# Layer 0's group norm: the root of 512 sums taken as 128 rows of 4, moved by transfers through DRAM

## The chip, the cores and the metric

The kernel runs on one core of a Trainium2 chip. The metric is device time in microseconds for one execution; the times are medians of several runs. The core has five engines with instruction queues of their own, each worked off in order: TensorE (PE in the profile, with its weight loads as PEld), VectorE (DVE), ScalarE (ACT), GpSimd (POOL) and SyncE (SP), which here only issues transfers.

## What is computed

A trunk of two layers over 1024 tokens of width 1024. Layer 0 mixes tokens by differential attention, layer 1 by latent attention; each is followed by a gated MLP with a causal convolution. The change lies in layer 0's attention, whose core is:

```python
def block(args):
    qb, blk = args
    sc = jnp.einsum('bqhcd,bkhcd->bhcqk', qb, k).astype(jnp.float32) * scale
    p = masked_softmax(sc, chunk_mask(blk, s)[None, None, None])
    a = p[:, :, 0] - lam * p[:, :, 1]
    return jnp.einsum('bhqk,bkhe->bqhe', a.astype(v.dtype), v)

o = from_blocks(lax.map(block, (to_blocks(q), jnp.arange(nb))))
o = rms_norm(o, subln_g) * (1.0 - lambda_init)
return o.reshape(b, s, D_MODEL) @ w_o
```

There are 8 heads; each has two softmaxes over the keys ("components"), subtracted with the weight lam. The group norm is the `rms_norm` over the 128 values of one head and one token: each value is divided by the root of the mean of the head's 128 squares plus 1e-6, then multiplied by a gain.

## The kernel before

The kernel is written with a tile framework: the program gives instructions in an order of priority, and a planner, which simulates the engines with costs of its own, sets the order on each engine and places all waits. Some regions are kept in the written order (`manual_schedule`), among them the part of the output projection in which PE and DVE run `project_rest`.

Values are 32-bit floats; to keep precision a matmul operand is split into a high part (`hi`, a rounded copy on ACT, L127) and a residue (`lo`, a subtraction on DVE or POOL, L130), and a product is three matmuls (`mm3`, L119 to L121).

Layer 0's attention goes through 32 steps: 8 heads with 4 pairs of query blocks each (p = 0 to 3, 256 queries in a step). `steps` interleaves them: in turn t it makes the scores and softmaxes of step t, turns and multiplies those of step t-1 by the values (`product`), and runs `finish` of step t-2. In between go the units that project the next queries, keys and values: they accumulate in the one PSUM bank "u" (L119 to L121 with `u<-s,s`), and are taken out by `rope` (shuffle L237, products L238 to L240) or, for values, by an ACT copy (L560). `weigh` divides the softmaxes by their sums: the reciprocal (L1578) on DVE, the second component's scale times -lam on ACT (L1579), the first component's rows on POOL or ACT (L147, L149), and their sum on DVE (L1581).

A half of a head's output, 128 values by 512 tokens, is complete after the steps p = 1 and p = 3; so there are 16 norms. `product` of such a step squares the output twice on ACT (L1599, L1600) and takes the residue on POOL (L130, `h<-h,h`). `finish`, a turn later, sums over the 128 rows by two matmuls with a matrix of ones (L1609, L1610), after which each of the 128 rows of the PSUM bank holds the same 512 sums; `rsqrt` (L170) takes 1 over the root of the whole 128x512 tile by Identity, Ln, Exp and Square on ACT (L174 to L177) and a correcting step on DVE (L178, L179); DVE multiplies with output and gain (L1613), and SP stores the tile to DRAM (L1614).

The tiles live in named places. The outputs `o` rotate over the places h2 and h3, and the tiles of the norm (squares, high part, residue, result, two temporaries) over the ring `fin` of h4 to h7. A tile that takes a place waits until all users of the tile before are done.

Elsewhere in the kernel the root of a norm is taken by POOL with a power of -0.5 (`root`, L167).

The output projection reads the stored halves back in blocks of 128 tokens (`project`, load L593, high part L127, residue L130): `project_first` with heads 0 to 3, which the planner may mix into the last attention steps, then `project_rest` with heads 4 to 7, in the order of blocks 0, 4, 1, 5, 2, 6, 3, 7. Block 4 is the first one that needs the second half of head 7. Weights are fetched by SP ahead of use (L135).

Of the kernel before, what the change touches and what calls it, by code (L numbers as in the profile page):

```python
# [10 lines left out]
F32 = mybir.dt.float32  # L11
F32R = mybir.dt.float32r
AF = mybir.ActivationFunctionType
ALU = mybir.AluOpType
# [4 lines left out]
P = 128  # L19
# [37 lines left out]
class Trunk:  # L57
# [40 lines left out]
    def ring(self, *places):  # L98
        return Ring(self, *places)
# [67 lines left out]
        nc.gpsimd.tensor_tensor(r, s, self.mhalf, ALU.pow)  # L167
        return r

    def rsqrt(self, ring, r, x, scale):  # L170

        nc = self.nc
        v, t = ring([P, 512]), ring([P, 512])
        nc.scalar.activation(v, x, AF.Identity, bias=self.eps, scale=scale)  # L174
        nc.scalar.activation(t, v, AF.Ln)
        nc.scalar.activation(r, t, AF.Exp, scale=-0.5)
        nc.scalar.activation(t, r, AF.Square)  # L177
        nc.vector.scalar_tensor_tensor(t, t, -0.5, v, ALU.mult, ALU.mult)  # L178
        nc.vector.scalar_tensor_tensor(r, t, 1.5, r, ALU.add, ALU.mult)  # L179

    def turn_blocks(self, src, dst):

        n = src.shape[-1] // P
        ps = self.bank()
        for k in range(n):
            self.nc.tensor.transpose(ps[:, k * P : (k + 1) * P], src[:, k * P : (k + 1) * P], self.ident)
        v = ps[:, : n * P].rearrange("p (k s) -> p k s", s=P)
        self.hi(dst(0), v)
        self.lo(dst(1), v, dst(0))
# [91 lines left out]
    def steps(self, attend, units, prepare, n, apart=False):  # L281


        steps = []
        for t in range(n + 2):
            now = before = None
            u = []
            if t < n:
                now = attend(t)
                steps.append(now)  # L290
                prepare(t)
                u = units(t)
                now.scores(0)
            if 0 < t <= n:
                before = steps[t - 1]
            alone = u[:-1] if apart else []
            if alone:
                u = u[-1:]
            self.run(alone or u, 2 if alone else 1)
            if before:  # L300
                before.turn()
            self.run(alone)
            if now:
                now.weigh(0)
                now.scores(1)
            self.run(u)
            if before:
                before.product()
            if now:
                now.weigh(1)  # L310
            if t >= 2:
                steps[t - 2].finish()


    def diff_attention(self, o_d, prefetch):
        nc, a = self.nc, self.a
# [5 lines left out]
        R = SimpleNamespace(  # L322
            k=self.ring("u0", "u1", "u2"), qh=self.ring("u3", "u4"), v=self.ring("u5", "u6", "u7"),
            P=self.ring("u8", "u9", "u10", "u11", "u12"), pT=self.ring("u13", "u14", "u15"),
            o=self.ring("h2", "h3"), fin=self.ring("h4", "h5", "h6", "h7"),
            rope=self.ring("h8", "h9", "h10", "h11"),
        )

# [25 lines left out]
        x, r = [], {}  # L354
# [1177 lines left out]
class DaStep(Step):  # L1532
# [40 lines left out]
    def weigh(self, j):  # L1573

        k, nc, l = self.k, self.k.nc, self.l[j]
        p0, p1 = self.probs[j]
        w = k.stat()
        nc.vector.reciprocal(l, l)  # L1578
        nc.scalar.mul(w, l[:, 1:2], k.neglam)  # L1579
        k.scale(p0, l[:, 0:1], "P" if self.p < 2 else "A")  # L1580
        nc.vector.scalar_tensor_tensor(p0, p1, w, p0, ALU.mult, ALU.add)  # L1581
        self.probs[j] = p0
# [20 lines left out]
    def finish(self):  # L1603

        k, nc = self.k, self.k.nc
        if not self.last:
            return
        ss = k.bank()
        nc.tensor.matmul(ss, k.ones, self.sl, start=True, stop=False)  # L1609
        nc.tensor.matmul(ss, k.ones, self.sh, start=False, stop=True)  # L1610
        r = self.R.fin([P, 512])
        k.rsqrt(self.R.fin, r, ss, 1.0 / P)
        nc.vector.scalar_tensor_tensor(r, self.o, k.g_sub, r, ALU.mult, ALU.mult)  # L1613
        nc.sync.dma_start(self.dst, r)  # L1614


class MlaStep(Step):
# [45 lines left out]
            nc.scalar.dma_start(self.dst, t)  # L1663

    def finish(self):
        pass


def kernel_body(tc, a, out):
    with ExitStack() as ctx:  # L1670
# [24 lines left out]
        def prefetcher(w_o, W, places, later):  # L1695


            raws = []
            half = KD // 2

            def step():
                while raws:
                    W.append(k.split(places[len(W)], raws.pop(0), nc.vector if len(W) % 2 else None))
                while len(W) + len(raws) < half and len(raws) < 2:
                    i = len(W) + len(raws)
                    raws.append(k.fetch(w_o[i * P : (i + 1) * P, :], D))

            def finish():
                while raws or len(W) < half:
                    step()  # L1710
                for i, place in zip(range(half, KD), later):
                    raws.append(k.at(place, [P, D]))
                    nc.sync.dma_start(raws[-1], w_o[i * P : (i + 1) * P, :])

            def rest():
                if raws:
                    W.append(k.split(places[len(W)], raws.pop(0), nc.vector))

            return step, finish, rest


        W = []
        step, finish, rest = prefetcher(a["da_w_o"], W, slots(*range(8)), units(10, 11, 12, 13))
        k.diff_attention(o_d[0], step)
        finish()
        first = {}

# [225 lines left out]
```

## Time and profile before

| | us |
|---|---|
| median of 3 runs (2431.1 to 2434.21) | 2432.36 |
| the profiled execution's own time | 2430.82 |
| its span, from the first to the last instruction | 2429.0 |
| PE busy, share of the span | 2361.7, 97% |
| DVE busy | 1899.3, 78% |
| ACT busy | 1304.4, 54% |
| POOL busy | 625.3, 26% |
| mean granted TensorE clock | 0.997 |

Times in the profile are counted from the span's start. A row of the timeline gives start, duration, engine, line, operation, tiles written and read, and in brackets how long the engine stood idle before, and what ended that wait. L with a number is the line of the kernel before. Busy time counts overlapping instructions of an engine once.

### The profile page before, as it was taken

The page shows a single profiled execution, that of the slowest core. Times are in us where ns is not written, and L with a number is a line of the kernel's source. Part 1 is how long each engine was busy: PE and PEld are TensorE (multiplying, and loading weights), DVE is VectorE, ACT ScalarE, POOL GpSimd, SP SyncE. Part 2 cuts the span into 40 slices and gives each one's busy share as a digit, 9 for nine tenths or more (in the row PEclk, how much of TensorE's full clock was granted, in tenths as well). Part 3 has the DMA queues.
Part 4 walks back from the last instruction along what each step waited for, and adds up shares of the span by engine and source line. Part 5 has one row for each costly group of instructions (what it writes and reads, how often), then busy time and mean ns, then how long its engine had stood idle before and what let it go on. Part 6 is the DMA issues. An engine that isn't in the chain of part 4 may idle for free. (4 is left out here: it accounts for less than half of the span.)

```text
span 2429.0 us, 32810 instructions
## 1 busy us (share of the span) xinstructions
PE 2361.7 (97%) x12032; PEld 2007.0 (83%) x12032; DVE 1899.3 (78%) x3094; ACT 1304.4 (54%) x2434; POOL 625.3 (26%) x500
## 2 busy tenths in 40 slices
PE   7999999999999999999999999999999999999998
PEld 6888878788888888878898788988888888887886
DVE  6677777756888888899964788886478888888997
ACT  5677776844444444444445777775344444444444
POOL 4545555425000000000042666664330000000001
PEclk9999999999999999999999999999999999999999
DMA  4111111333222222553221211123322222227502
GB/s 161 47 37 36 35 36 44 100 100 126 70 78 83 83 80 93 194 175 120 84 90 55 68 40 40 40 76 119 108 70 87 78 88 86 78 87 277 171 3 79
DMA packets 95793, 213.93 MB, mean 88 GB/s; under 512 B 8720, under 2 KB 33936, under 8 KB 95632
## 3 DMA queue, kind: packets, MB, share of 16 engines
q1 hardware_dynamic: 86448, 184.04, 22.9%
q10 hardware_dynamic: 9184, 27.79, 3.1%
q8 instruction: 95, 1.56, 0.3%
q14 instruction: 66, 0.54, 0.1%
HBM read 159.37 MB, written 52.43 MB: 87 GB/s over the span
## 5 line engine op out<-in xcount | busy, mean ns | idle before, releaser
L167 POOL TENSOR_TENSOR st<-st,mhalf 128x1 f32<-128x1 f32 x56 | 35.7, 638 | 1311.7 <-DVE st L164 1306.7
L127 ACT CAST u<-h 128x512 fp32r<-128x512 f32 (+2 forms) x242 | 146.1, 619 | 280.2 <-DVE h L779 260.1
L119 PE MATMUL S<-s,u 128*128 128x512 f32 (+1 forms) x752 | 286.0, 380 | 0.7 <-DVE s L130 0.5
L120 PE MATMUL S<-s,u 128*128 128x512 f32 (+1 forms) x752 | 284.6, 379 | 0.0
L121 PE MATMUL S<-s,u 128*128 128x512 f32 (+1 forms) x752 | 284.6, 378 | 0.0
L119 PE MATMUL b<-s,u 128*128 128x512 f32 x588 | 230.8, 392 | 2.1 <-DVE S L1635 1.0
L121 PE MATMUL b<-s,u 128*128 128x512 f32 x588 | 229.2, 390 | 0.0
L120 PE MATMUL b<-s,u 128*128 128x512 f32 x588 | 229.2, 390 | 0.0
L836 DVE SCALAR_TENSOR_TENSOR u<-u,conv,u 128x1023 f32<-128x1023 f32 (+1 forms) x176 | 224.7, 1277 | 1.6 <-ACT u L832 1.6
L149 POOL TENSOR_TENSOR u<-u,st 128x384 f32<-128x384 f32 (+7 forms) x160 | 169.2, 1067 | 151.4 <-DVE st L1643 107.8
L127 ACT CAST s<-u 128x512 fp32r<-128x512 f32 (+2 forms) x202 | 128.8, 673 | 110.4 <-PE u L121 35.9
L119 PE MATMUL u<-s,s 128*128 128x512 f32 (+1 forms) x440 | 176.7, 402 | 11.1 <-DVE h L238 4.5
L130 DVE TENSOR_TENSOR u<-b,u 128x512 fp32r<-128x512 f32 (+1 forms) x256 | 157.7, 629 | 24.3 <-ACT u L127 22.4
L121 PE MATMUL u<-s,s 128*128 128x512 f32 (+1 forms) x440 | 172.9, 393 | 0.0
L120 PE MATMUL u<-s,s 128*128 128x512 f32 (+1 forms) x440 | 172.2, 391 | 0.0
L119 PEld LDWEIGHTS S<-s,u 128*128 128x128 f32 x752 | 141.8, 189 | 27.9 <-DVE s L130 0.9
L121 PEld LDWEIGHTS S<-s,u 128*128 128x128 f32 x752 | 141.9, 189 | 26.2
L120 PEld LDWEIGHTS S<-s,u 128*128 128x128 f32 x752 | 141.9, 189 | 26.0
L127 ACT CAST u<-b 128x512 fp32r<-128x512 f32 (+1 forms) x256 | 133.5, 549 | 28.1 <-PE b L252 22.3
L839 ACT ACTIVATE u<-u 128x1024 f32<-128x1024 f32 x44 | 46.8, 1062 | 187.5 <-DVE u L836 187.5
L130 DVE TENSOR_TENSOR s<-u,s 128x512 fp32r<-128x512 f32 (+2 forms) x187 | 127.4, 714 | 17.7 <-ACT s L127 17.6
L130 DVE TENSOR_TENSOR u<-h,u 128x512 fp32r<-128x512 f32 x166 | 114.1, 687 | 32.4 <-ACT u L127 31.5
(263 smaller groups left out, 6632.1 us busy)
## 6 DMA issues: line engine op xcount, KB each, us to landing
u<-in_ffn_up SPq DMA_DIRECT2D x88, 512.0 KB, 3.9
g_d<-u ACTq DMA_DIRECT2D x44, 512.0 KB, 2.6
u<-in_ffn_down SPq DMA_DIRECT2D x66, 256.0 KB, 4.7
u<-g_d SPq DMA_DIRECT2D x62, 256.0 KB, 4.3
s<-in_da_wqkv SPq DMA_DIRECT2D x23, 512.0 KB, 3.3
x_d<-u SPq DMA_DIRECT2D x16, 512.0 KB, 3.0
s<-x_d SPq DMA_DIRECT2D x8, 1024.0 KB, 10.5
u<-o_d SPq DMA_DIRECT2D x24, 256.0 KB, 2.9
```

The lines of the kernel that those rows point to most:

```text
L119: mm(out, lh, rl, start=first, stop=False, skip_group_check=onto)
L120: mm(out, lh, rh, start=False, stop=False, skip_group_check=onto)
L121: mm(out, ll, rh, start=False, stop=last, skip_group_check=onto)
L127: self.nc.scalar.copy(out, src)
L130: (eng or self.nc.vector).tensor_sub(out, src, hi.bitcast(F32))
L149: self.nc.gpsimd.tensor_mul(x, x, s.to_broadcast(list(x.shape)))
L167: nc.gpsimd.tensor_tensor(r, s, self.mhalf, ALU.pow)
L836: nc.vector.scalar_tensor_tensor(t[half][:, back:], u[half][:, : S - back], w, t[half][:, back:], ALU.mult, ALU.add)
L839: nc.scalar.activation(t[0], t[0], AF.Silu)
```

## The change

The function `rsqrt` goes. `finish` now takes only one row of the sums out of PSUM, with the mean and the epsilon (ACT), stores the 512 values to DRAM, loads them back as 128 rows of 4 into the first four columns of the result tile, takes the power of -0.5 of these on POOL, stores the 512 roots to DRAM, and loads them spread over all 128 partitions. All four transfers are issued by SP. The product with output and gain and the store move into a new function `complete`, which `steps` runs one turn later than `finish`, so that the loop has one turn more (in latent attention both functions do nothing). The outputs get a third place (h4), and the ring `fin` has three places instead of four, for five tiles of a norm instead of six. In `weigh` the second component's scale is a DVE product instead of an ACT one.

```diff
@@ steps
-        for t in range(n + 2):
+        for t in range(n + 3):
...
-            if t >= 2:
+            if 2 <= t < n + 2:
                 steps[t - 2].finish()
+            if t >= 3:
+                steps[t - 3].complete()
@@ diff_attention
-            o=self.ring("h2", "h3"), fin=self.ring("h4", "h5", "h6", "h7"),
+            o=self.ring("h2", "h3", "h4"), fin=self.ring("h5", "h6", "h7"),
@@ DaStep.weigh
         nc.vector.reciprocal(l, l)
-        nc.scalar.mul(w, l[:, 1:2], k.neglam)
+        nc.vector.tensor_mul(w, l[:, 1:2], k.neglam)
@@ DaStep.finish
         ss = k.bank()
         nc.tensor.matmul(ss, k.ones, self.sl, start=True, stop=False)
         nc.tensor.matmul(ss, k.ones, self.sh, start=False, stop=True)
-        r = self.R.fin([P, 512])
-        k.rsqrt(self.R.fin, r, ss, 1.0 / P)
-        nc.vector.scalar_tensor_tensor(r, self.o, k.g_sub, r, ALU.mult, ALU.mult)
-        nc.sync.dma_start(self.dst, r)
+        row = self.R.fin([1, 512])
+        nc.scalar.activation(row, ss[0:1], AF.Identity, bias=k.eps[0:1], scale=1.0 / P)
+        sums, roots = (k.dr.tile([1, 512], F32, name=k.name("roots")) for _ in range(2))
+        across = lambda x: x.rearrange("o (p c) -> (o p) c", c=4)
+        self.r = self.R.fin([P, 512])
+        c = self.r[:, 0:4]
+        nc.sync.dma_start(sums, row)
+        nc.sync.dma_start(c, across(sums))
+        nc.gpsimd.tensor_tensor(c, c, k.mhalf.to_broadcast([P, 4]), ALU.pow)
+        nc.sync.dma_start(across(roots), c)
+        nc.sync.dma_start(self.r, roots.partition_broadcast(P))
+
+    def complete(self):
+        k, nc = self.k, self.k.nc
+        if not self.last:
+            return
+        nc.vector.scalar_tensor_tensor(self.r, self.o, k.g_sub, self.r, ALU.mult, ALU.mult)
+        nc.sync.dma_start(self.dst, self.r)
```

More of the change, by code (lines that the diff above doesn't have):

```diff
@@ L168, in root @@
         return r
[L170 to L179, printed above, removed]
     def turn_blocks(self, src, dst):
@@ L1665, in finish, with complete @@
     def finish(self):
+        pass
+    def complete(self):
         pass
```

## The prediction

> **What bounds the kernel now.** I read the busy time by stretches first, then who made PE wait there, then the timeline of all engines where layer 0's attention ends. The change lies in layer 0's attention alone: from 85 us, when the first sum of squares is at hand, to 537 us, where the output projection takes over. In the second row below the columns are the stretch, its length, then busy time and count of PE, PEld, DVE, ACT and POOL, the granted clock, DMA share and GB/s.
>
> ```profile
> span 2429.0 us, 32810 instructions
> 85.00:537.00 452.00, 436.71 (x2347) 370.53 (x2345) 321.88 (x556) 322.76 (x669) 213.20 (x152) 1.00 0.16 54
> ```
>
> PE is busy 436.71 of 452.00 us and the clock is full. So PE sets this stage's time, ACT (71%), DVE (71%) and POOL (47%) have room, and the most that lighter engines can win is PE's idle time, 15.3 us. The largest causes of it (waiter, waited for, total us, times, longest):
>
> ```profile
> PE u L119 <- ACT h L560: 4.2, 4, 1.3
> PE S L1553 <- ACT u L1568: 3.6, 3, 1.5
> PE u L119 <- DVE h L238: 2.3, 5, 0.6
> PE b L252 <- ACT h L174: 0.8, 1, 0.8
> ```
>
> ACT ends 8.6 us of it, DVE less. Next the end of the stage: the last norm (head 7, second half) and the first projection block that needs it.
>
> ```profile
> 521.05 1.29 POOL L130 TENSOR_TENSOR h<-h,h 128x512 fp32r<-128x512 f32 x1 [6.88 <-ACT h L1600]
> 526.16 0.40 PE L1609 MATMUL b<-h,ones 128*128 128x512 f32 x1
> 526.39 0.39 PE L1610 MATMUL b<-h,ones 128*128 128x512 f32 x1
> 526.88 0.69 ACT L174 ACTIVATE h<-b,eps 128x512 f32<-128x512 f32 x1 [4.10 <-PE b L1610]
> 531.10 0.75 DVE L1613 SCALAR_TENSOR_TENSOR h<-h,g_sub,h 128x512 f32<-128x512 f32 x1
> 531.88 0.33 SPq L1614 DMA_DIRECT2D o_d<-h  x1
> 534.46 0.36 SPq L593 DMA_DIRECT2D u<-o_d  x1
> 536.85 0.39 PE L121 MATMUL S<-s,h 128*128 128x512 f32 x1
> 537.20 1.14 ACT L127 CAST h<-u 128x512 fp32r<-128x512 f32 x2 [7.64 <-DMA u<-o_d]
> 537.87 0.50 PE L119 MATMUL S<-s,h 128*128 128x512 f32 x1 [0.64 <-ACT h L127]
> 539.23 0.50 PE L121 MATMUL S<-s,h 128*128 128x512 f32 x1 [0.62 <-POOL h L130]
> ```
>
> The norm goes matmul, ACT, DVE, store, load, cast, matmul with no slack: PE already waits 0.64 us for the cast and ACT waited 7.64 us for the load. Whatever lengthens the norm here reaches PE in full. The 15 norms before this one are not read until later, so their length is covered by PE's other work.
>
> **What the change takes off and puts on.** Rows: busy us and mean ns of one.
>
> ```profile
> L175 ACT ACTIVATE h<-h 128x512 f32<-128x512 f32 x16 | 10.2, 635 | 0.2
> L177 ACT ACTIVATE h<-h 128x512 f32<-128x512 f32 x16 | 10.2, 636 | 0.2
> L178 DVE SCALAR_TENSOR_TENSOR h<-h,h 128x512 f32<-128x512 f32 x16 | 11.8, 741 | 6.1 <-ACT h L177 6.0
> L179 DVE SCALAR_TENSOR_TENSOR h<-h,h 128x512 f32<-128x512 f32 x16 | 14.5, 907 | 0.3
> L1579 ACT ACTIVATE st<-st,neglam 128x1 f32<-128x1 f32 x64 | 19.0, 302 | 13.4 <-DVE st L1578 13.2
> L167 POOL TENSOR_TENSOR st<-st,mhalf 128x1 f32<-128x1 f32 x56 | 35.7, 638 | 1311.7 <-DVE st L164 1306.7 <-PE b L186 3.8 <-DVE st L166 1.1
> L1596 ACT COPY h<-b 128x256 f32<-128x256 f32 x32 | 11.7, 367 | 5.2 <-PE b L121 5.2
> L1660 ACT COPY h<-u 64x256 f32<-64x256 f32 x64 | 23.6, 369 | 11.0 <-PE u L1658 9.8
> L164 DVE TENSOR_SCALAR st<-st 128x1 f32<-128x1 f32 x55 | 8.2, 150 | 50.8 <-ACT u L157 50.3 <-ACT h L157 0.2
> L228 DVE TENSOR_TENSOR neglam<-st x1: 527/527/527, 48.9 to 48.9; 128x1 f32<-128x1 f32 x1
> ```
>
> ACT loses three activations for each of 16 norms (3 x 10.2 = 30.6 us) and the 64 small multiplications (19.0 us): 49.6 us. Its first activation stays; it works on one row now, but 64 and 128 partitions cost the same here (369 and 367 ns), so I leave it at 0.69 us. DVE loses 11.8 + 14.5 = 26.3 us and gains 64 multiplications of 128x1, between 150 ns (a 128x1 operation with a constant) and 527 ns (one with two tensors, seen once): 9.6 to 33.7 us. I take 150 ns, which the 55 repeated ones show. POOL gains 16 roots of 128x4. The 128x1 root takes 638 ns; four times that, 2.6 us, is the upper end. I take 0.7 us, as such small work is mostly fixed cost: 11 us in all on an engine that is half idle. SP gains four transfers for each norm, 64 in all.
>
> **The end of the stage: +5.2 us.** The three activations and two DVE steps that go lie between the end of L174 (526.88 + 0.69 = 527.57) and the start of L1613 (531.10): 3.5 us. In their place come, each waiting for the one before: the row to DRAM (2 KB), 128 rows of 4 back (2 KB), the root, the roots to DRAM (2 KB), and the row spread over 128 partitions (256 KB written). None of this size stands alone in the trace; the nearest (KB, us from issue to landing):
>
> ```profile
> o_d<-h SPq DMA_DIRECT2D x16, 256.0 KB, 2.0
> x_d<-u SPq DMA_DIRECT2D x16, 512.0 KB, 3.0
> s<-o_d SPq DMA_DIRECT2D x8, 256.0 KB, 2.9
> ```
>
> For a small store the upper end is the 256 KB store, 2.0 us; the line through 256 and 512 KB (2.0 and 3.0 us) gives 1.0 us at no size, the lower end; I take 1.5. For the small load 1.0 to 2.9 us; I take 2.0. For the spread load 2.0 to 2.9; I take 2.8, nearest the load of the same size. Sum: 1.5 + 2.0 + 0.7 + 1.5 + 2.8 = 8.5 us, and 0.2 for five hand-overs of about 0.03 us (DVE ends at 531.85, SP issues at 531.88) and more for POOL: 8.7 - 3.5 = +5.2 us. The ends are 5.6 - 3.5 = +2.1 and 12.4 - 3.5 = +8.9 us. POOL has nothing to do there, as its cast residue is held by the same load, and SP's next issue is that load. [...]
>
> **The other 15 norms: -3.0 us.** Where PE waits for ACT, work that goes stands ahead of what PE needs:
>
> ```profile
> 276.02 0.62 ACT L177 ACTIVATE h<-h 128x512 f32<-128x512 f32 x1
> 277.84 0.29 ACT L1579 ACTIVATE st<-st,neglam 128x1 f32<-128x1 f32 x1
> 279.08 0.56 ACT L560 COPY h<-u 128x512 f32<-128x512 f32 x1
> 279.69 0.51 PE L119 MATMUL u<-s,s 128*128 128x512 f32 x1 [0.85 <-ACT h L560]
> 314.41 0.64 ACT L175 ACTIVATE h<-h 128x512 f32<-128x512 f32 x1
> 315.57 0.50 PE L119 MATMUL u<-s,s 128*128 128x512 f32 x1 [1.33 <-ACT h L560]
> ```
>
> Without 0.62 + 0.29 us ahead of it the first copy ends PE's 0.85 us; the second wait falls by about 0.64 of 1.33. That is 1.49 of 2.18 us; the same share of L560's 4.2 us is 2.9, say 3.0. The ends are 0 (the planner orders all engines anew and other waits appear) and all 15.3 us.
>
> **New waits: +1.5 us.** Two engines that serve PE now wait for transfers in their own order: POOL in front of the root (behind it rotary steps, weight splits and row scales), and DVE in front of the last product with the spread roots (behind it rotary, maxima and splits). SP, too, holds later weight fetches behind a load that waits for its store. What such a wait costs is seen where ACT waits for a fetch that SP issued late:
>
> ```profile
> ACT s L127 <- DMA u<-in_da_w_o: 10.5, 4, 3.7
> SPq L135 <- POOL s L130: 153.5, 16, 26.6
> ```
>
> 2.6 us each. ACT's idle time in the stage is 452.0 - 322.8 = 129 us, of which 8.6 reached PE, 7%. Sixteen such waits at 2.6 us and 7% are 2.9 us, none is 0; I take half. One more wait: three buffers serve what four did, so the residue of the next squares is written where the spread roots of the norm before lie until stored. The shortest distance now:
>
> ```profile
> 248.91 0.45 PE L1609 MATMUL b<-h,ones 128*128 128x512 f32 x1
> 261.76 1.29 POOL L130 TENSOR_TENSOR h<-h,h 128x512 fp32r<-128x512 f32 x1 [4.15 <-ACT h L1600]
> ```
>
> 12.85 us, against 0.7 + 0.7 + 8.7 + 0.75 + 2.0 = 12.85 for the new norm up to its landed store. It fits just so, and with queues it is a us or two late; POOL waits 4.15 us before it already, and it counts among the sixteen.
>
> The scale moved to DVE saves a hand-over behind the reciprocal, too; I put no own gain on it, as its reader L1581 is not among the causes of PE's waits. Later stages keep their code and their waits.
>
> **Sum.** +5.2 - 3.0 + 1.5 = +3.7 us on the profiled 2430.82 us (span 2429.0 and 1.8 around it). The median of the runs is 2432.36, 1.5 above the profiled one; I add the 3.7 there: 2436.1, rounded 2436.0. A measurement can tell about 0.2%, 4.9 us, from no change, so this is no change that can be told, on its slow side.
>
> **Rivals.** (a) *DVE stands behind the transfers: slower.* The mechanism is the in-order wait at the last product, 16 times 2.6 us = 42 us, with a fifth of it reaching PE instead of 7%, since with DVE at 71% a late evacuation holds the single accumulator bank that L119 waits for (L238). That is 8.4 us in place of 1.5: +10.6, 2443. For: SP waits 153.5 us for POOL in front of fetches, up to 26.6 at once, and a norm's transfers queued behind such a fetch come that much late. Against: PE waited for DVE's L238 only 2.3 us so far. It decides from a share of 7% on, where the sum passes +4.9. (b) *The lighter ACT wins and the end is covered: faster.* At the end the residue is ready at 522.34 but its matmul starts at 526.16, 3.8 us later, with other projection matmuls first. If the planner puts it ahead, the seam costs +1.4; if 9.5 of PE's 15.3 us go, the sum is about -8, 2424. Against: only the 8.6 us of ACT waits are touched at all. (c) *The end is covered, little else moves:* +1.4 - 3.0 = -1.6 and no new waits, 2431.
>
> **How the numbers follow.** Forecast 0.52, with own range 2434 to 2439: the unknown transfers put three parts in seven of it above +4.9. (a) 0.23, (b) 0.15, (c) 0.10. Slower: 0.23 + 0.22 = 0.45; same: 0.30 + 0.10 = 0.40; faster: 0.15. The range 2426 to 2446 takes in the forecast and (c) whole, half of (a)'s and (b)'s spread, and leaves out 0.19.
>
> **What would show it.** Right: between L1610 and the first matmul of the second projection block PE's wait grows from 0.64 us to 5 to 6, the four transfers take 1.5 to 2.8 us each, PE's idle time before 521 us falls to 11 to 14 us, ACT's busy time falls by 50 us, DVE's by 17. Wrong: PE's idle time before 521 us above 17 us with DVE or POOL waiting for a DMA ahead of it (a), or no long wait at the second block (b, c).

## The result and the profile after

| | before | after |
|---|---|---|
| median of 6 runs, us | 2433.14 (2431.02 to 2434.55) | 2455.52 (2446.33 to 2461.04) |
| profiled execution, us | 2430.82 | 2450.86 |

The change makes the kernel slower: ratio 1.0093, 95% interval 1.0077 to 1.0108. That is 22 us where 3.7 were forecast, and outside the range. In the views from here on, L is a line of the kernel that the view is of. The answer of the profile by cores (span, mean granted TensorE clock) for after; before stood at 0.997:

```profile
core 0: 2449.1 us, clock 0.992
```

The six runs of the same program follow this clock: 2446.33 us at 0.994, 2450.86 at 0.992, 2454.80 and 2456.24 at 0.991, 2460.89 and 2461.04 at 0.989. Fifteen microseconds lie between executions of one and the same instruction order.

I first asked where the 20.0 us between the two profiled executions arise, by the times of the same instructions in both traces:

| place | after minus before, us |
|---|---|
| 57 us, before the first norm | +2.7 |
| output sum of block 4, the second block of the output projection (545.2 and 559.0) | +13.8 |
| first maximum of layer 1's attention (1327.4 and 1339.1) | +11.7 |
| last maximum of layer 1's attention (1671.3 and 1693.3) | +22.0 |
| end | +20.1 |

The first 2.7 us are a stretch of half clock ahead of the change (50 to 57 us, granted clock 0.52); the kernel before shows the same stretch in a later run (with a barrier, below; 0.54), so it isn't the change's. The rest arises in two places: layer 0's attention up to the second projection block, and **layer 1's attention, whose code is not changed**. The busy times by stretches (stretch, length, busy us and count of PE, PEld, DVE, ACT, POOL, granted clock, DMA share, GB/s), for after:

```profile
85.00:537.00 452.00, 434.68 (x2330) 369.71 (x2329) 333.89 (x584) 289.13 (x568) 224.49 (x168) 0.99 0.20 61
510.00:556.00 46.00, 35.64 (x155) 29.02 (x154) 16.37 (x17) 11.94 (x19) 10.38 (x9) 0.89 0.30 92
518.00:521.40 3.40, 3.40 (x19) 3.40 (x18) 2.21 (x4) 1.28 (x2) 0.00 (x0) 0.52 0.68 231
549.50:556.50 7.00, 5.63 (x15) 4.02 (x16) 1.67 (x1) 0.62 (x1) 1.28 (x1) 0.58 0.38 124
1339.00:1747.00 408.00, 393.55 (x2400) 345.31 (x2401) 298.40 (x695) 274.61 (x592) 235.64 (x187) 0.99 0.21 63
```

ACT got lighter in the first row (289 against 323 us) and PE didn't get faster. The clock column is new: the prediction read a full clock in before and had no term for a change of it. From 518 and 549 us on PE runs at about half speed for 3.4 and 6.8 us (0.52 and 0.58 in the rows; the second row runs past its stretch, which is at 0.53 from 549.0 to 555.8 us). Who makes PE wait, and how long DVE and POOL wait for roots, after, 40 to 620 us (waiter, waited for, total us, times, longest):

```profile
PE u L119 <- DVE h L227: 10.8, 9, 1.6
PE S L119 <- ACT h L127: 6.6, 1, 6.6
PE b L241 <- DVE u L130: 4.1, 2, 3.6
PE u L119 <- ACT h L551: 0.2, 1, 0.2
DVE h L1618 <- DMA h<-roots: 39.8, 15, 4.4
POOL h L1610 <- DMA h<-roots: 13.5, 4, 6.1
```

The 6.6 us is the one place where layer 0's attention ends. Its timeline, after:

```profile
533.75 0.68 ACT L1603 ACTIVATE h<-b,eps 1x512 f32<-1x512 f32 x1 [3.70 <-PE b L1601]
534.46 0.24 SPq L1608 DMA_DIRECT2D roots<-h  x1
535.63 0.34 SPq L1609 DMA_DIRECT2D h<-roots  x1
537.50 1.01 POOL L1610 TENSOR_TENSOR h<-h,mhalf 128x4 f32<-128x4 f32 x1 [5.52 <-DMA h<-roots]
538.53 0.33 SPq L1611 DMA_DIRECT2D roots<-h  x1
540.33 0.32 SPq L1612 DMA_DIRECT2D h<-roots  x1
544.07 0.75 DVE L1618 SCALAR_TENSOR_TENSOR h<-h,g_sub,h 128x512 f32<-128x512 f32 x1 [4.14 <-DMA h<-roots]
544.85 0.32 SPq L1619 DMA_DIRECT2D o_d<-h  x1
546.86 0.37 SPq L584 DMA_DIRECT2D u<-o_d  x1
550.06 0.62 ACT L127 CAST h<-u 128x512 fp32r<-128x512 f32 x1 [2.93 <-DMA u<-o_d]
550.74 0.80 PE L119 MATMUL S<-s,h 128*128 128x512 f32 x1 [6.63 <-ACT h L127]
```

Each step starts as the one before lands: 1.17 us for the row's store, 1.87 for the 128 rows of 4, 1.01 for the root, 1.80 for the roots' store, 3.74 for the spread load: 9.6 us from L1608 to L1618. The matmul behind the wait takes 0.80 us where the same form took 0.39 before it.

The other DVE wait, L227, is not behind a transfer. Four of its nine, 1.43 to 1.51 us each, stand where DVE and POOL work side by side, once in each of four heads. After, around 215 us:

```profile
214.97 2.39 POOL L130 TENSOR_TENSOR s<-s,s 128x1024 fp32r<-128x1024 f32 x1 [4.03 <-ACT s L127]
215.11 3.20 DVE L1572 SCALAR_TENSOR_TENSOR u<-u,st,u 128x896 f32<-128x896 f32 x1
218.86 0.67 DVE L227 TENSOR_TENSOR h<-u,s 128x512 f32<-128x512 f32 x1
219.58 0.50 PE L119 MATMUL u<-s,s 128*128 128x512 f32 x1 [1.47 <-DVE h L227]
```

L1572 needs 3.20 us for 896 columns while POOL's subtraction runs; alone, the same form takes 1.15 us in the kernel before. What is new is their place in the order: four of the eight take 3.20 to 3.37 us here, while the slowest two in the kernel before take 2.27.

### The profile page after: what moved, and what is told of

It is laid out like the page before. It is cut to its first block, busy times and chain, and to the rows that moved or that the text cites. A ratio compares the mean times of both kernels' runs of the same rounds, so it can differ in the third digit from the quotient of the medians.

```text
span 2449.1 us, 32868 instructions
## 1 busy us (share of the span) xinstructions
PE 2372.3 (97%) x12032; PEld 2012.6 (82%) x12032; DVE 1912.0 (78%) x3126; ACT 1266.8 (52%) x2322; POOL 636.0 (26%) x516
## 3 DMA queue, kind: packets, MB, share of 16 engines
q1 hardware_dynamic: 93392, 188.33, 23.4%
## 4 chain that ended last, share of the span: by engine, by line
PE 79%; DVE 8%; DMA 5%; ACT 3%; POOL 3%; issue 2%; SPq 0%; DVEq 0%; POOLq 0%; ACTq 0%
PE S L119 13%; PE S L121 13%; PE S L120 13%; PE b L119 8%; PE b L120 8%; PE b L121 8%; PE u L119 3%; PE u L120 3%; PE u L121 3%; PE b L241 2%; DMA h<-roots 1%; PE u L1663 1%; DVE u L1572 1%; PE u L1662 1%; PE b L175 1%
## 5 line engine op out<-in xcount | busy, mean ns | idle before, releaser
L130 DVE TENSOR_TENSOR u<-b,u 128x512 fp32r<-128x512 f32 (+1 forms) x256 | 157.9, 631 | 27.0 <-ACT u L127 24.4
L241 PE MATMUL b<-ident,u 128*128 128x128 f32 x864 | 139.1, 278 | 12.5 <-DVE u L130 9.0
L130 DVE TENSOR_TENSOR s<-u,s 128x512 fp32r<-128x512 f32 (+2 forms) x187 | 127.6, 715 | 22.2 <-ACT s L127 22.1
```

Source lines behind the costliest of these rows:

```text
L130: (eng or self.nc.vector).tensor_sub(out, src, hi.bitcast(F32))
L241: self.nc.tensor.transpose(ps[:, j * P : (j + 1) * P], probs[t][:, k : k + P], self.ident)
```

## The experiments

Theory A, as it stood after the first four runs: the loss has three parts that the sum lacked or undersized. The planner orders layer 1's attention anew whenever layer 0's attention is edited; the end of layer 0's attention gets a long wait, from the chain of transfers or because projection matmuls that covered the norm go ahead of it; and the clock halves behind long waits. Theory B: norms through DRAM cost wherever they stand, because DVE and POOL wait for them in order. The texts on record give the rest.

All kernels in one table. "85 to block 4" is the stretch from 85 us to block 4's output sum with PE's busy and idle time in it; "cover" is the time from the last sum of squares to the first output sum, "wait" PE's longest wait for the second block's cast, and layer 1 the time from the first to the last maximum of its attention. Ratios are to runs of the kernel before beside each kernel's own. The lengths of after and of e11_bar_before hold the 2.7 us that both lost before 57 us.

| kernel | median us | ratio (95%) | 85 to block 4: length, PE busy, idle | cover | wait | layer 1 |
|---|---|---|---|---|---|---|
| before | 2433.1 | 1 | 460.2, 443.7, 16.6 | 11.1 | 0.6 | 343.9 |
| after | 2455.5 | 1.0093 (1.0077 to 1.0108) | 474.0, 449.9, 24.1 | 11.7 | 6.6 | 354.2 |
| e1_scale | 2449.7 | 1.0074 (1.0057 to 1.009) | 467.3, 446.3, 21.0 | 6.1 | 6.9 | 354.2 |
| e2_norm | 2454.4 | 1.009 (1.0071 to 1.0109) | 475.4, 450.2, 25.2 | 5.7 | 12.3 | 354.0 |
| e3_delay | 2448.8 | 1.007 (1.0051 to 1.009) | 466.3, 445.1, 21.2 | 5.9 | 6.8 | 352.2 |
| e4_late | 2450.6 | 1.0076 (1.0055 to 1.0096) | 470.0, 447.0, 23.0 | 11.8 | 6.8 | 353.1 |
| e5_late2 | 2435.9 | 1.0011 (1.0003 to 1.002) | 462.9, 444.5, 18.4 | 11.1 | 0.4 | 345.7 |
| e6_act57 | 2430.0 | 0.9987 (0.9978 to 0.9996) | 456.8, 444.0, 12.8 | 11.1 | 0.6 | 345.4 |
| e7_act_p3 | 2446.6 | 1.0054 (1.004 to 1.0069) | 474.6, 451.2, 23.4 | 14.3 | 3.4 | 345.7 |
| e8_last_old | 2448.6 | 1.0062 (1.0049 to 1.0074) | 468.0, 449.4, 18.6 | 11.1 | 0.8 | 354.1 |
| e9_act14 | 2439.7 | 1.0034 (1.0021 to 1.0047) | 469.5, 447.8, 21.7 | 11.1 | 0.6 | 346.5 |
| e10_bar_after | 2452.9 | 1.0089 (1.0075 to 1.0103) | 471.3, 448.3, 23.0 | 11.8 | 6.8 | 341.4 |
| e11_bar_before | 2445.7 | 1.0052 (1.0039 to 1.0066) | 462.5, 446.1, 16.4 | 11.1 | 0.6 | 342.4 |

PE executes 2146 instructions between the first and the last maximum of layer 1's attention. By line and tile, the traces have them in one and the same order in before, e5, e6, e7 and e9, and in one other order in after and e1 to e4; e8's differs from that one in 8 places. The two barrier kernels share an order of their own, with 2115 instructions between the maxima, so that their 341 to 342 us can be set beside each other alone.

**e1_scale**: the kernel before with one line changed.

```diff
-        nc.scalar.mul(w, l[:, 1:2], k.neglam)
+        nc.vector.tensor_mul(w, l[:, 1:2], k.neglam)
```

> The kernel before with one edit: the second component's scale on VectorE instead of ScalarE; no transfer through DRAM, no third output place, the norm as before. In the planned order of the instructions, layer 1's attention stands on PE and ACT exactly as in the changed kernel, though none of its code differs from before. Theory A (half of the loss is that order of layer 1's attention, 10 us; the rest is the exposed chain of transfers where layer 0's attention ends, and half-speed clock after PE's waits): the stretch of layer 1's attention is 8 to 11 us longer than before, PE's wait at the second projection block stays under 1.5 us, and the whole is 5 to 11 us slower (2438 to 2444). Rival B (the loss is DVE's waits for the spread roots in layer 0, and layer 1's 10 us were a chance of that execution): within 3 us of before.

Four fifths of the loss come with this one line, without a single new transfer. The scale itself isn't the price: it takes 22.7 us of DVE in all 64 places. PE's waits between 530 and 570 us, e1_scale:

```profile
PE S L119 <- ACT h L127: 6.9, 1, 6.9
```

Here the norm is the old, short one. But the planner now runs 24 projection matmuls ahead of the last sum of squares that stood behind it, so the cover shrinks from 11.1 to 6.1 us and the wait is as long as with the chain. I had not expected this wait, and the total is 6 us above A's range. And layer 1's attention takes 354.2 us, as in the changed kernel, though nothing of it is edited.

**e2_norm**: the changed kernel with the scale back on ACT.

```diff
-        nc.vector.tensor_mul(w, l[:, 1:2], k.neglam)
+        nc.scalar.mul(w, l[:, 1:2], k.neglam)
```

> The changed kernel with the scale back on ScalarE: the norm through DRAM alone. Layer 1's attention stands on PE and ACT as in the changed kernel. Theory A: layer 1's attention 8 to 11 us longer than before, PE's wait at the second projection block 5 to 7 us, the whole 12 to 24 us slower than before, as the changed kernel is. Rival B: the same total, but layer 1's attention within 2 us of before and more than 10 us in layer 0 before 520 us.

The cover is lost and the chain is there, and the two add: PE's wait at the same place, e2_norm:

```profile
PE S L119 <- ACT h L127: 12.3, 1, 12.3
```

That is twice the wait that A had; its total and its time of layer 1 came true. Up to there the norms through DRAM do pay: between 400 and 450 us of before, DVE's maxima come about 8 us earlier.

**e3_delay**: the changed kernel (loop, rings, `complete` a turn later, scale on DVE) with the old root and no transfer through DRAM.

```diff
-        row = self.R.fin([1, 512])
...
-        nc.sync.dma_start(self.r, roots.partition_broadcast(P))
+        self.r = self.R.fin([P, 512])
+        k.rsqrt(self.R.fin, self.r, ss, 1.0 / P)
```

> The changed kernel without its transfers: frame, third output place, three places for the norm's tiles, last product a turn later, and the scale on VectorE, but the root by the old activations and DVE steps on the whole tile. Theory A: layer 1's attention 8 to 11 us longer than before, PE's wait at the second projection block under 1.5 us, the whole 5 to 12 us slower than before and 8 to 14 us faster than the changed kernel. Rival B: within 3 us of before.

No transfers, cover lost, a wait of 6.8 us, 352.2 us in layer 1: 2448.8 us. The wait was again not expected (A had under 1.5), and the kernel is 17.5 us slower than before where A had 5 to 12. Without what the title of the change names, most of the loss is still there. Theory B can't be the whole of it.

**e4_late**: the changed kernel with `complete` another turn later.

```diff
-        for t in range(n + 3):
+        for t in range(n + 4):
...
-            if t >= 3:
-                steps[t - 3].complete()
+            if t >= 4:
+                steps[t - 4].complete()
```

> The changed kernel with the last product and the store two turns after the root is asked for instead of one, so that the roots have landed when DVE comes to them. Rival B: DVE's waits for the roots (39.8 us in the changed kernel) fall under 10 us, and the whole becomes 8 us faster than the changed kernel or more. Theory A: DVE's waits fall as much, but the whole moves by less than 4 us, since only one PE wait of 3.6 us stood behind them, and the chain at the end stays.

DVE's waits, e4_late, 85 to 560 us:

```profile
DVE h L1618 <- DMA h<-roots: 45.7, 16, 5.4
```

A turn more in the written order doesn't keep DVE from waiting: the planner places the product by its own due times, and the waits rose from 39.8 to 45.7 us. Both theories had them fall, so that was a miss. The time is a few microseconds below the changed kernel's, within its spread.

For the next kernels I kept some norms the old way and chose which ones so that the compiled order of layer 1's attention comes out as before's or not:

```diff
+        if CONDITION:
+            self.r = self.R.fin([P, 512])
+            k.rsqrt(self.R.fin, self.r, ss, 1.0 / P)
+            return
         row = self.R.fin([1, 512])
```

**e5_late2**: CONDITION is `self.p == 3 and self.h >= 6`.

> The changed kernel, but the second norm of heads 6 and 7 (two of 16) the old way; 14 norms still go through DRAM and the scale stays on VectorE. In its compiled program TensorE's order in layer 1's attention is again that of the kernel before, and 24 more projection matmuls stand behind the last sum of squares than in the one-line edit, as in the kernel before. Theory A (the loss is the planner's new order in layer 1, the long chain or the lost cover at the one place where layer 0's attention ends, and the clock halved behind the waits): layer 1's attention takes 342 to 346 us instead of 354, no wait over 2 us at the second projection block, 2425 to 2433 us in all. Theory B (every norm through DRAM costs, by waits behind transfers, as rival (a) of the prediction): 14 of 16 norms still pay, 2446 or more.

Fourteen norms through DRAM and the scale on DVE cost 0.1%. The median is 3 us above what A gave at most, and 10 below B's least. One of its eleven executions took 5141 us, for a reason that isn't known; the others lie between 2432.6 and 2440.7. Layer 1's attention, before and then e5_late2:

```profile
1327.00:1725.00 398.00, 388.43 (x2400) 343.35 (x2401) 298.37 (x696) 274.73 (x592) 236.07 (x187) 1.00 0.21 64
```

```profile
1330.50:1729.00 398.50, 388.39 (x2396) 343.59 (x2397) 297.45 (x693) 274.14 (x591) 235.69 (x186) 0.99 0.21 64
```

**e6_act57**: scale on ACT, CONDITION `self.h in (5, 7)`.

> The changed kernel with the scale on ScalarE and both norms of heads 5 and 7 the old way: 12 norms go through DRAM. TensorE's order in layer 1's attention and around the last sum of squares is that of the kernel before in the compiled program. Theory A: layer 1's attention 342 to 346 us, no wait over 2 us at the second block, and the relief of ScalarE that the run with the norm alone showed by 425 us (7.7 us) for 12/16: about 5; 2424 to 2428 us, below the kernel before by over 0.2%. Theory B: 12 of 16 norms pay, 2443 or more.

2430.0 us, the only kernel of the study below before (2433.0 beside it), by 0.13% (interval 0.04 to 0.22%), where 2424 to 2428 had been expected. PE's idle time up to block 4 falls from 16.6 to 12.8 us; layer 1 takes back 1.5 us. So the norm through DRAM can win a little. The old order of layer 1 is not enough for it: e7 and e9 have that order, too, and lose.

**e7_act_p3**: scale on ACT, CONDITION `self.p == 3 and self.h < 6`; the last norm goes through DRAM with more cover (14.3 us).

> The changed kernel with the scale on ScalarE and the second norm of heads 0 to 5 the old way: 10 norms through DRAM, the last one among them. TensorE's order in layer 1's attention is that of the kernel before; behind the last sum of squares stand 14 more projection matmuls than there. Theory A: layer 1's attention 342 to 346 us; at the second block a wait of 2 to 5 us, less than the 6.6 of the changed kernel, as the chain of 9.6 us has more cover; in all 2426 to 2432. Theory B: 10 of 16 norms pay, 2442 or more.

Layer 1 (345.7) and the wait at the second block (3.4) came as A had it, the total didn't: it is 15 us above A's range and within B's (2442 or more). The loss stands earlier, and it is theory B's mechanism. Around 177 us, e7_act_p3:

```profile
173.47 2.34 POOL L130 TENSOR_TENSOR s<-s,s 128x1024 fp32r<-128x1024 f32 x1 [3.75 <-ACT s L127]
173.51 2.84 DVE L1633 SCALAR_TENSOR_TENSOR h<-h,g_sub,h 128x512 f32<-128x512 f32 x1 [3.41 <-DMA h<-roots]
176.28 1.27 DVE L130 TENSOR_TENSOR u<-b,u 128x512 fp32r<-128x512 f32 x2
177.01 0.90 PE L252 MATMUL b<-ident,u 128*128 128x128 f32 x3 [4.70 <-DVE u L130]
```

DVE waits for the spread roots, its product is then slow beside a POOL subtraction (2.84 us; 0.75 for the same line in e9 below), and the split L130 behind it is what PE's transposes need: PE waits 4.70 us at 177.0, and the clock is at half speed for 6.8 us from 175 us on (granted 0.52).

**e8_last_old**: the changed kernel, CONDITION `self.h == DA_HEADS - 1 and self.p == 3`, only the last norm the old way.

> The changed kernel with the one norm that ends layer 0's attention (head 7, second half) the old way; 15 go through DRAM, the scale stays on VectorE. Behind the last sum of squares stand as many projection matmuls as in the changed kernel. TensorE's order in layer 1's attention is a third one, neither that of before nor of the changed kernel, and its price is not known. Theory A: the wait at the second block falls from 6.6 to under 1.5 us, and no half-speed stretch of the clock follows it; the part up to the second block is 6 to 9 us shorter than in the changed kernel; layer 1's attention between 344 and 355 us; 2431 to 2444 in all. Theory B: 15 of 16 norms pay, and the wait at the second block goes to another place: 2450 or more.

PE's waits between 530 and 570 us, e8_last_old:

```profile
PE S L119 <- ACT h L127: 0.8, 1, 0.8
PE S L121 <- POOL h L130: 0.6, 1, 0.6
```

With the cover as in the changed kernel and the old norm at this one place, the wait falls from 6.6 to 0.8 us: the chain of four transfers makes the changed kernel's wait. The total fell by 7 us only (median), and 2448.6 is above A's 2444 and under B's 2450: layer 1 stands at 354.1, and the first stretch is still 7.8 us longer than before. That stretch splits cleanly, as it holds as many PE instructions as in before (2375; before's row, then e8_last_old's, with two of its slow windows):

```profile
85.00:545.20 460.20, 443.65 (x2375) 375.81 (x2374) 324.50 (x560) 325.68 (x674) 216.36 (x156) 1.00 0.17 55
```

```profile
85.00:553.00 468.00, 449.38 (x2375) 379.29 (x2374) 331.47 (x589) 293.39 (x571) 230.37 (x171) 0.99 0.21 63
456.00:459.40 3.40, 3.36 (x14) 2.96 (x13) 3.35 (x9) 2.21 (x5) 2.46 (x3) 0.51 0.26 95
490.50:497.30 6.80, 6.37 (x16) 5.00 (x17) 3.43 (x7) 1.98 (x3) 1.41 (x1) 0.52 0.47 155
```

PE idles 2.1 us more (18.6 against 16.6) and is busy 5.7 us more with the same instructions. The clock is enough for the second part. By the granted clock of these windows (0.51 and 0.52) PE does up to 1.7 us less work in 3.4 us, by estimate; four such windows (275, 456 and two from 490 us) give 6.8 at most.

**e9_act14**: scale on ACT, CONDITION `(self.h, self.p) in ((4, 1), (7, 3))`.

> The changed kernel with the scale on ScalarE and only two of the 16 norms the old way (head 4, first half, and the last one, head 7, second half); 14 go through DRAM, as in the run with heads 6 and 7. In the compiled program the order of layer 1's attention is that of the kernel before on TensorE, VectorE and ScalarE, and as many projection matmuls stand behind the last sum of squares. Theory A: layer 1's attention 343 to 346 us, no wait over 2 us at the second block, relief of 5 to 8 us by 425 us; 2424 to 2431 us in all, 4 to 8 below the run with 14 norms and the scale on VectorE (2435.9), which prices the moved scale. Theory B (norms through DRAM cost wherever they stand): above the kernel with 12 norms, 2433 or more.

Missed, too: 2439.7 is in B's range (2433 or more). Layer 1 (346.5) and the second block (0.6) are as before's, and by 350 us the kernel is 7 us ahead. Then, e9_act14:

```profile
387.53 0.32 SPq L1627 DMA_DIRECT2D h<-roots  x1
392.56 0.75 DVE L1633 SCALAR_TENSOR_TENSOR h<-h,g_sub,h 128x512 f32<-128x512 f32 x1 [6.35 <-DMA h<-roots]
395.04 1.89 DVE L130 TENSOR_TENSOR u<-b,u 128x512 fp32r<-128x512 f32 x3
395.79 0.90 PE L252 MATMUL b<-ident,u 128*128 128x128 f32 x3 [5.65 <-DVE u L130]
```

The spread roots, issued at 387.53, reach DVE 5.0 us later. Its one wait for them becomes 5.65 us of PE's and two windows of half clock (394 to 401 us, granted 0.53); by 400 to 450 us the lead is gone. So this run, meant to price the moved scale against e5_late2, can't: the planner's order differs in more than the scale. The price of the moved scale by itself stays open.

**e10_bar_after and e11_bar_before**: one line ahead of layer 1's attention heads, in the changed kernel and in the kernel before.

```diff
+        tc.strict_bb_all_engine_barrier()
         heads.rest(step)
```

> The changed kernel whole (16 norms through DRAM, scale on VectorE), with a barrier of all engines between layer 0's tail and layer 1's attention heads, so that the planner orders layer 1's attention from there anew; its TensorE order there is the same as in the kernel before with the same barrier. Theory A (half of the loss is layer 1's order): over the kernel before with the barrier it is 8 to 14 us slower, what the changed kernel had lost by 600 us, and layer 1's attention takes the same time in both within 2 us. Rival (the loss in layer 1 comes from transfers, memory or the clock, not from the order): 18 to 24 us slower, 8 to 10 of them in layer 1's attention.

> The kernel before with the same barrier and nothing else: the partner of the run before this one. Both theories: slower than without the barrier by what a drain of all engines costs, 3 to 15 us, with its own length of layer 1's attention; only the difference of the two barrier kernels tells the theories apart.

Layer 1's attention, e10_bar_after, then e11_bar_before:

```profile
1349.80:1744.10 394.30, 383.04 (x2367) 337.26 (x2366) 292.03 (x684) 267.19 (x576) 230.73 (x182) 1.00 0.20 61
```

```profile
1345.20:1740.40 395.20, 382.56 (x2366) 337.08 (x2365) 292.41 (x683) 266.94 (x576) 230.74 (x182) 1.00 0.20 61
```

With one and the same order in layer 1 the whole change costs 2452.9 - 2445.7 = 7.2 us, not 22 (runs of 2451.4 to 2457.4 and of 2442.5 to 2447.2). That is a little under A's 8 to 14, and far from the rival's 18 to 24; layer 1 differs by 1 us. The loss of layer 1 is the planner's order; e1 and e3, which have it without any transfer, leave the transfers out as its cause. The barrier itself costs 13.8 us (2445.7 against 2431.9), so it mends nothing.

## Why the prediction was wrong

**The step that failed is the last sentence of its working, "Later stages keep their code and their waits".** They keep their code. Their order is the planner's, and it can change with an edit in layer 0's attention: 352 to 354 us in place of 344 in the changed kernel and in e1 to e4 and e8, 345 to 347 in e5, e6, e7 and e9, where the order on TensorE is before's. This term is +10 us of the 20 and stood in the sum with 0. The prediction let the planner's new order cost something in its own stage (the end 0 of the relief) and nothing behind it. Where it goes is seen in PE's waits there (after, 1339 to 1747 us):

```profile
PE b L241 <- DVE u L130: 4.9, 10, 0.9
PE S L119 <- ACT u L1642: 2.2, 3, 1.8
PE b L241 <- DVE S L1640: 1.2, 1, 1.2
```

The first of these was 1.7 us in three waits before, the second 0.8. In all PE idles 5 us more, and it is busy 5 us more with the same 2400 instructions (393.6 against 388.4); one window of half clock at 1637 us (0.50 over 3.4 us) explains 1.7 of that, the other 3 or so are not explained. The clock isn't the cause: between the two maxima e2 has as much half clock as before, 3.4 us, and takes 354.0. Which part of the new order costs the time stays open.

**The clock had no term at all.** A wait of PE was priced at its length. In the changed kernel three waits of layer 0 (1.52, 3.60 and 6.63 us) have half clock beside them, 13.7 us up to block 4 at a granted clock of 0.50 to 0.52, in which PE does, by estimate, up to 6.8 us less work; its busy time up to there rose by 6.2. In e8 above the clock cost more than the added waiting. Layer 0's attention lost 11.1 us in all (13.8 less the 2.7) where the sum had 3.7.

**The end of the stage, +5.2 us:** right in its mechanism, close in size. The wait grew from 0.64 to 6.63 us, where 5 to 6 had been said; the chain took 9.6 us and not 8.7. Undersized were the root (1.01 against 0.7; the medians are 1.02 us for four columns and 0.55 for the 128x1 root, and the line through both has 0.39 at no column) and the spread load (3.74 against 2.8, beyond its end of 2.9); oversized the first store (1.17 against 1.5). The four transfers take 8.58 us together, singly 1.17 to 3.74. e8_last_old shows that this chain makes the wait. The forecast missed that the cover of 11 us is itself the planner's choice: with it gone the wait is there without any transfer (e1, e3).

**Relief of ACT, -3.0 us:** the instructions removed and added take 50.1 us off ACT by groups (49.6 expected), though its busy time, which counts overlaps once, fell by 37.6 (1304.4 to 1266.8) where 50 had been said. PE's wait for the value copy (L560 before, L551 after) went from 4.2 to 0.2 us. Between 400 and 425 us the changed kernel stands 0.4 us ahead of before, so that it has won 3.1 us since the 2.7 lost by 57. With the scale on ACT, e2 and e6 won about 8 by then. So ACT's relief is real and was undersized, and new waits take it back before the stage ends: four for L227 (5.8 us in all), 1.52 for the norm's ACT step at 454.84 and 3.60 at 516.87. PE's idle time from 85 to 537 us, all of it before 521, rose from 15.3 to 17.3 us, where 11 to 14 had been said. That is just above the 17 that was to be the sign of rival (a).

**New waits, +1.5 us, and rival (a):** DVE waited 39.8 us for roots in 15 waits, where the rival had 16 times 2.6. At one place it reaches PE in the changed kernel: DVE's product waits 2.48 us at 514.87, its split L130 starts at 516.14, and PE waits 3.6 us at 516.87. That is 9% of DVE's waits, close to the 7% of the sum, with a window of half clock behind it. The fifth that the rival had did not reach PE here; in e7 one wait alone was 4.7 of 27.5 us. Rival (a)'s mechanism is real, and e7 and e9 show it, too; its price is set by the place. Here it gave 3.6 of the 20 us and the half clock behind them. Rival (b), a lighter ACT and a covered end, is what e6 shows, with a win of 3 us and not of 8, once four norms are kept the old way.

**DVE's scale:** all 64 of after (min, median and max ns), then groups of after, 85 to 550 us:

```profile
L1570 DVE TENSOR_TENSOR st<-st,neglam x64: 153/160/2257, 53.6 to 502.7; 128x1 f32<-128x1 f32 x64
```

```profile
L1570 DVE TENSOR_TENSOR st<-st,neglam 128x1 f32<-128x1 f32 x59 | 27.9, 472 | 1.5
L1603 ACT ACTIVATE h<-b,eps 1x512 f32<-1x512 f32 x16 | 10.8, 678 | 5.9 <-PE b L1601 5.8
```

By itself one takes 153 to 160 ns, as the 150 of the sum had it. The mean is 472 because 22 of the 64 take 0.4 to 2.3 us, and each of these ends within 0.03 us of the end of a POOL instruction beside it (the last section has more of this). What the sum missed is that DVE waits for POOL here. So DVE's busy time rose by 12.7 us over the span (1899.3 to 1912.0) instead of falling by 17: the 64 scales add 29.9 us and not 9.6, and the eight L1572 of 896 columns add 7.6. One row costs ACT as much as 128 (678 ns, and 687 for L174 in before, both medians), as assumed.

## What to carry to other kernels

Where a planner orders the program, an edit in one stage can be paid in another that it doesn't touch. Compare the compiled order of the later stages first, and price an edit between two kernels that have the same order there; here a barrier pair gave 7 us where the plain comparison gave 22.

Here the end of a stage with one reader was the place where the chain of transfers counted: PE waited 6.6 us there, and 0.8 with the old norm in its place (e8). Fourteen norms elsewhere cost 0.1% in e5; where DVE waited for the roots ahead of something that PE needs, one wait cost PE 4.70 us (e7) and 5.65 (e9). Look for that one place, not for the sum of the waits.

A stall of the matmul engine of over 2.2 us had half clock behind it in 51 of 59 cases here, and so cost more than its length: read the granted clock behind a stall.

A mean can mix two kinds of the same instruction. Read the median beside it, and look for what runs beside the slow ones.

## What the hardware showed

Half-clock stretches last 3.4 us (three in before, five in after) or 6.8 us (two in after), at a granted clock of 0.50 to 0.53, but for the last one, which runs out with the program (0.50 from 2422.6 us on in before). I counted PE's waits over 1 us between 85 and 2420 us in the thirteen profiles, and for how many of them half clock set in during the wait or within 3.5 us of its end:

| PE's wait, us | number | with half clock behind it |
|---|---|---|
| 1.0 to 1.5 | 54 | 0 |
| 1.5 to 2.2 | 77 | 21 |
| 2.2 to 3.0 | 25 | 19 |
| over 3.0 | 34 | 32 |

Half clock stands behind waits well under 3.4 us, too: behind 21 of the 77 of 1.5 to 2.2 us, and behind none of the 54 shorter ones. Why one wait of 2 us has it behind it and another hasn't is not shown; the runs show the spread (2446 to 2461 us for one program, at mean clocks of 0.994 to 0.989), not its cause.

DVE's sum of the two softmaxes and POOL's subtraction hold each other up where they run side by side (3.20 us against 1.15, 3.23 against 2.39). L1572 by its columns, groups of after, 85 to 550 us, and then the first form in before:

```profile
L1572 DVE SCALAR_TENSOR_TENSOR u<-u,st,u 128x896 f32<-128x896 f32 x8 | 19.2, 2403 | 0.0
L1572 DVE SCALAR_TENSOR_TENSOR u<-u,st,u 128x1024 f32<-128x1024 f32 x8 | 11.2, 1405 | 1.4 <-ACT u L147 1.2
```

```profile
L1581 DVE SCALAR_TENSOR_TENSOR u<-u,st,u 128x896 f32<-128x896 f32 x8 | 11.6, 1451 | 3.8 <-ACT u L147 3.8
```

One of the form with POOL idle (before), and POOL's subtraction where DVE's sum of 896 columns began first, at 159.91 (after):

```profile
212.04 1.15 DVE L1581 SCALAR_TENSOR_TENSOR u<-u,st,u 128x896 f32<-128x896 f32 x1 [1.66 <-ACT u L147]
```

```profile
160.07 3.23 POOL L130 TENSOR_TENSOR s<-s,s 128x1024 fp32r<-128x1024 f32 x1 [4.48 <-ACT s L127]
```

Fewer columns take longer in after, 2403 ns against 1405 in the mean, as four of the eight take 3.20 to 3.37 us beside a POOL subtraction. In the timeline of 215 us above POOL begins at 214.97 and ends at 217.36, DVE begins at 215.11 and ends at 218.31, 0.95 us after POOL: not much less than the 1.15 us that the work takes alone. At 159.91 DVE took 1.14 us, and POOL 3.23 in place of 2.39. In these two places the one that began first took its time alone and the other was held; why is not shown. At 384.16 DVE is recorded 0.02 us ahead of POOL and is still the one held (3.37 us, POOL 2.40), so a start so close doesn't tell who goes first. So where the planner puts POOL's subtraction beside the sum of the two softmaxes, DVE loses about 2 us (3.20 against 1.15), and PE waits some 1.5 us for a rotary step (L227) in each of four heads.
